# Toeplitz tiles of a causal convolution: fetched ready-made from DRAM instead of being multiplied out by GpSimd

## The chip, the cores and the metric

The kernel runs on one core of one Trainium2 chip. The metric is device time in microseconds (us) of one launch. A profile of one execution stands beside the times; all durations below come from it. Engines are called as the profile calls them: PE (TensorE, matmuls), PEld (its weight loads), DVE (VectorE), ACT (ScalarE), POOL (GpSimd), SP (SyncE, which issues most DMAs). L1809 is line 1809 of the kernel before.

## What is computed

A stack of layers on a sequence of 512 tokens and 1024 channels in fp32: a feed-forward block, a mixer of linear-recurrent heads and attention, a second feed-forward block, an "even" layer (pooling and a state-space scan), and an "odd" layer, whose mixer is cut down here to what matters:

```python
def _odd_mixer(h, w_in, conv_w, conv_b, ln_g, ln_b, w_out):
    proj = h @ w_in
    val, gt, z = proj[..., :1024], proj[..., 1024:2048], proj[..., 2048:]
    g = val * sigmoid(gt)
    c = depthwise_conv(g, conv_w, taps=31, left_pad=30) + conv_b   # per channel, causal
    c = layer_norm(c) * ln_g + ln_b
    return (silu(c) * silu(z)) @ w_out
```

The convolution has 31 taps for each of the 1024 channels. Everything has to keep fp32 accuracy, so that matrix products are done as three products of split operands (a high part `wh`, `h` and a low part `wl`), at L134, L135 and L136.

## The kernel before

The 1024 channels are 8 blocks of 128. The odd layer convolves them in two ways. Blocks 0 to 3 go tap by tap on DVE: `conv_dve` issues one instruction for tap 0 (L1786) and 30 multiply-adds (L1789, tile `cn`) for each block; these are dripped in between other work, and the layer's weight splits stand in the same in-order DVE queue (SP loads a raw tile `wr`, of which there are four buffers; L115 on ACT makes `wh` of it, L116 on DVE `wl`). Blocks 4 to 7 (`PE_BLOCKS`) go to PE as products with Toeplitz tiles: for each of the four groups of 32 channels of a block a tile `L` of 128 partitions by 36 x 32 numbers holds the taps, shifted by the phase of its partition, among zeros; 9 matmuls (L1812) run over slices of it against `G`, the flipped block. There are 16 such tiles, in four buffers (`LB` = 4), so that the four tiles of one block can be made while the block before is multiplied and no earlier than its matmuls let go of the buffers.

Before, a tile is made in two steps. During the second feed-forward block (`ffn2`), a list of side steps is taken up now and then between the matmuls; `odd_setup` is the first on it. For each of the four PE blocks it zeroes a tile on DVE (L1769), loads the taps of the block four times, shifted, by small DMAs from the ACT queue (L1772), transposes them with four PE instructions (L1776) and copies the result from PSUM (L1778) to a table `wtab`. Later, in the odd layer, POOL multiplies this table, spread over 32 columns, with a 0/1 pattern `i32` (L1809): 16 instructions of 128 x 1152 numbers, each giving one `L`. On POOL's in-order queue between them stand four additions `tot` (L1898, L1900), which sum convolved blocks for the mean of the layer norm, and small memsets of `G` (L1797).

The order in the odd layer is written out by hand (`ODD_PLAN`): `f` a block for DVE, `P6` and `P4` a projection of two PE blocks with tokens on partitions (token-major: one split weight tile serves 12 matmuls), `G` a flip, `C6`, `C7`, `C4`, `C5` the matmuls with the Toeplitz tiles, `O` the way back, `z` a gate block. After it come the mean (L1904), the layer norm (L1907, L1917) and the output projection.

The first thing in the odd layer is the norm of its input: the sums of squares (L266 on ACT, L270 on DVE) and a product with ones on PE (L284). The memory for the first four `L` comes free when the even layer's last matmuls are done.

Of the kernel before, what the change touches and what calls it, by code (L numbers as in the profile page):

```python
# [14 lines left out]
ALU = mybir.AluOpType  # L15
# [3 lines left out]
P = 128  # L19
S = 512  # L20
D = 1024
NB = D // P
# [1687 lines left out]
TAPS = 31  # L1710
# [6 lines left out]
NI = 36  # L1717
PE_BLOCKS = (4, 5, 6, 7)
# [23 lines left out]
        return R, r  # L1742


def odd_consts():
    m = (np.arange(P)[:, None] % 32 == np.arange(32)[None, :]).astype(np.float32)
    return {"k_i32": m}


def odd_setup(g, ins):  # L1750
    nc = g.nc
    g.i32 = g.c([P, 32], "i32")
    nc.scalar.dma_start(g.i32[:], ins["k_i32"])
    cw = ins["conv_w_2"].rearrange("o k c -> (o k) c")
    rows = cw.rearrange("k (b p) -> (k b) p", p=P)
    g.cw = g.c([P, TAPS, NB], "cw")
    flatw = g.cw[:].rearrange("p k b -> p (k b)")
    for i in range(2):
        t = g.b()
        nc.scalar.dma_start(t[:124, :P], rows[i * 124:(i + 1) * 124, :])  # L1760
        yield
        p = g.paux()
        nc.tensor.transpose(p[:, :124], t[:124, :P], g.ident[:124, :124])
        nc.vector.tensor_copy(flatw[:, i * 124:(i + 1) * 124], p[:, :124])
        yield
    g.wtab = {}
    for b in PE_BLOCKS:
        t = g.b()
        nc.vector.memset(t[:NI], 0.0)  # L1769
        t4 = t[:].rearrange("i (q j c) -> i q j c", q=4, j=4)  # L1770
        for j in range(4):
            nc.scalar.dma_start(t4[5 - j:36 - j, :, j, :], cw[:, b * P:(b + 1) * P].rearrange("k (q c) -> k q c", q=4))  # L1772
        yield
        p = g.paux()
        for q in range(4):
            nc.tensor.transpose(p[:, q * NI:(q + 1) * NI], t[:NI, q * P:(q + 1) * P], g.ident[:NI, :NI])  # L1776
        w = g.c([P, 4 * NI], f"wtab{b}")
        nc.vector.tensor_copy(w[:], p[:, :4 * NI])  # L1778
        g.wtab[b] = w
        yield  # L1780


def conv_dve(g, b, gp, cs):
# [19 lines left out]
def conv_pe(g, b, G):  # L1803
    nc = g.nc
    p = g.pacc()
    for q in range(4):
        L = g.X.tile([P, NI, 32], F32, tag="L", name=g.name("L"), bufs=LB)
        w = g.wtab[b][:, q * NI:(q + 1) * NI]
        nc.gpsimd.tensor_tensor(L[:], w[:, :, None].to_broadcast([P, NI, 32]), g.i32[:, None, :].to_broadcast([P, NI, 32]), ALU.mult)  # L1809
        for dc in range(9):  # L1810
            lw = L[:, (8 - dc) * 4:(8 - dc) * 4 + 4, :].rearrange("p j c -> p (j c)")
            nc.tensor.matmul(p[:, q * P:(q + 1) * P], lhsT=G[:, q, 8 - dc:8 - dc + P], rhs=lw, start=(dc == 0), stop=(dc == 8))  # L1812
    t = g.b()
    nc.scalar.activation(t[:].rearrange("p (j q c) -> p q j c", j=4, q=4), p[:].rearrange("p (q j c) -> p q j c", j=4, q=4), AF.Copy)
    return t
# [9 lines left out]
def odd(g, ins, nrm, after):  # L1825
# [51 lines left out]
    def step(op, b):  # L1877
        if op == "f":
            fm_block(b)
        elif op == "z":  # L1880
            z_block(b)
        elif op == "P":
            Zs[b // 2] = pair(b)
        elif op == "G":
            Gs[b] = conv_flip(g, b, Zs[b // 2])
        elif op == "C":
            Gs[b] = conv_pe(g, b, Gs[b])
            drip(DP)
        else:
            cs[b] = conv_out(g, b, Gs.pop(b))  # L1890
# [87 lines left out]

def all_consts():
    d = {"k_ident": np.eye(P, dtype=np.float32)}  # L1980
    for f in (mix_consts, ssm_consts, odd_consts):
        d.update(f())
    return d

# [4 lines left out]
def build(g, ins, out):  # L1989
    nc = g.nc  # L1990
    with g.region("mixc") as mixc:
        with g.region("ffn1", ring=True):
            nrm = part1(g, ins, {2: lambda: mix_loads(g, ins, mixc), 5: lambda: mix_tables(g, mixc)})
        a3 = scale_cols(g, "a3", "g_ffn2", 7)
        nrm3 = ModNorm(g, lambda: a3, modvec(g, 6))
        with g.region("mix", ring=True):
            mixer1(g, ins, nrm, modvec(g, 5), nrm3.add)
    gt3 = half_gate(g, "gt3", 8)
    with g.region("evp") as evp:
        m = Ssm(evp)  # L2000
        with g.region("ffn2", ring=True):
            def side():
                yield from odd_setup(g, ins)
                yield from ssm_prep(g, ins, m)

            nrm = EvenNorm(g)
            ffn(g, None, ins["w_gu2"], ins["w_down2"], lambda: gt3, side(), nrm.add, (0, 8, 15, 22), rate=2, side_later=PREP_LATER, nrm=nrm3)
        nrm6 = PlainNorm(g, g.cols["odd_norm_2"])
        with g.region("evm", side="left"):
            even(g, ins, nrm, m, nrm6.add)  # L2010
    with g.region("odd", side="left"):
        fin = Final(g, out)
        odd(g, ins, nrm6, fin.add)
# [18 lines left out]
```

## Time and profile before

| | |
|---|---|
| time, median of 3 runs | 1532.93 us (1531.78 to 1533.9) |
| the profiled execution's own time | 1530.95 us |
| its span, first to last instruction | 1529.2 us |
| PE busy | 1465.4 us (96%) |
| DVE busy | 1064.8 us (70%) |
| ACT busy | 637.9 us (42%) |
| POOL busy | 110.9 us (7%) |
| mean granted TensorE clock | 0.981 of full speed |

Busy time of PE is close to the span, so the time is PE's own work plus the places where PE stands still or runs at the lower clock. To read such a profile one asks first for PE's waits over the whole program, then for what the engine that PE waited for was doing, and then for the rows of the instructions that the change touches.

### The profile page before, as it was taken

What the parts mean: (1) busy time and instruction counts of PE and PEld (TensorE: products, weight loads), DVE (VectorE), ACT (ScalarE), POOL (GpSimd) and SP (SyncE); (2) the same over time, 40 slices, a digit from 0 to 9 for tenths busy, and PEclk for the clock granted to TensorE, in tenths of its full rate; (3) what the DMA queues carried; (4) which work ended last, traced back from release to release, by engine and by line L of the source; (5) the groups of instructions that cost most, each with busy time, mean ns of one, the idle gap of its engine ahead of it and who ended that gap; (6) DMA issues with size and microseconds to landing.
All of it is one profiled execution on the core that took longest, in us unless ns stands there. A gap on an engine that the chain in (4) does not pass through costs nothing.

```text
span 1529.2 us, 20513 instructions
## 1 busy us (share of the span) xinstructions
PE 1465.4 (96%) x7258; PEld 1221.0 (80%) x7258; DVE 1064.8 (70%) x2284; ACT 637.9 (42%) x1176; POOL 110.9 (7%) x118
## 2 busy tenths in 40 slices
PE   3899999999999999999999999999999998989997
PEld 3788888888987877789778888888888887869777
DVE  6885664564575687867339749946589757998975
ACT  5333223333365657845322332235434543313365
POOL 2211000000000002010000001000000002025100
PEclk7999999999999999999999999999999999999999
DMA  9498663643222213023323422332213232311121
GB/s 334 122 316 238 201 200 115 199 145 91 75 84 76 70 54 85 8 69 89 106 86 90 117 83 83 104 90 87 86 49 97 65 94 83 97 49 56 56 69 70
DMA packets 240267, 163.94 MB, mean 107 GB/s; under 512 B 18636, under 2 KB 220588, under 8 KB 240164
## 3 DMA queue, kind: packets, MB, share of 16 engines
q1 hardware_dynamic: 230260, 159.64, 34.4%
q0 software_dynamic: 1424, 1.75, 0.6%
q10 hardware_dynamic: 8480, 1.24, 0.5%
q8 instruction: 57, 0.93, 0.3%
q14 instruction: 46, 0.38, 0.1%
HBM read 159.51 MB, written 2.10 MB: 106 GB/s over the span
## 4 chain that ended last, share of the span: by engine, by line
PE 80%; DVE 12%; ACT 3%; issue 2%; DMA 2%; SPq 0%; ACTq 0%; DVEq 0%
PE pa L136 23%; PE pa L135 23%; PE pa L134 23%; DVE cn L1789 4%; DVE wl L116 1%; PE px L1076 1%; PE px L873 1%; PE px L865 1%; DVE adah L443 1%; PE pa L1812 1%; ACT wh L115 0%; DMA xt<-in_x 0%; DMA g<-in_w_gu 0%; PE px L481 0%; PE px L291 0%
## 5 line engine op out<-in xcount | busy, mean ns | idle before, releaser
L115 ACT ACTIVATE wh<-wr 128x512 fp32r<-128x512 f32 (+1 forms) x444 | 274.8, 626 | 621.4 <-PE pa L135 410.3
L116 DVE TENSOR_TENSOR wl<-wr,wh 128x512 fp32r<-128x512 f32 (+1 forms) x444 | 303.2, 688 | 242.1 <-ACT wh L115 241.1
L134 PE MATMUL pa<-h,wh 128*128 128x512 f32 (+1 forms) x1144 | 433.3, 381 | 6.1 <-ACT h L115 6.0
L136 PE MATMUL pa<-h,wl 128*128 128x512 f32 (+1 forms) x1144 | 431.1, 378 | 3.3 <-DVE wl L116 3.3
L135 PE MATMUL pa<-h,wh 128*128 128x512 f32 (+1 forms) x1144 | 431.5, 378 | 1.5 <-DVE h L116 1.5
L134 PEld LDWEIGHTS pa<-h,wh 128*128 128x128 f32 x1144 | 216.1, 189 | 45.0 <-ACT h L115 6.5
L136 PEld LDWEIGHTS pa<-h,wl 128*128 128x128 f32 x1144 | 216.4, 189 | 42.3 <-DVE wl L116 4.2
L135 PEld LDWEIGHTS pa<-h,wh 128*128 128x128 f32 x1144 | 216.9, 190 | 41.3 <-DVE h L116 3.4
L134 PE MATMUL pa<-g,wh 128*128 128x512 f32 (+1 forms) x374 | 142.3, 380 | 0.0
L135 PE MATMUL pa<-g,wh 128*128 128x512 f32 (+1 forms) x374 | 142.1, 380 | 0.0
L136 PE MATMUL pa<-g,wl 128*128 128x512 f32 (+1 forms) x374 | 141.9, 379 | 0.0
L135 PE MATMUL pa<-wl,h 128*128 128x512 f32 x256 | 102.4, 400 | 7.4 <-DVE wl L116 7.4
L1789 DVE SCALAR_TENSOR_TENSOR cn<-gp,cw,cn 128x512 f32<-128x512 f32 x120 | 105.3, 905 | 1.4
L134 PE MATMUL pa<-wh,h 128*128 128x512 f32 x256 | 103.1, 403 | 0.6 <-DVE p L1068 0.6
L136 PE MATMUL pa<-wh,h 128*128 128x512 f32 x256 | 101.6, 398 | 0.0
L136 PEld LDWEIGHTS pa<-g,wl 128*128 128x128 f32 x374 | 70.4, 188 | 12.9
L135 PEld LDWEIGHTS pa<-g,wh 128*128 128x128 f32 x374 | 70.4, 188 | 12.9
L134 PEld LDWEIGHTS pa<-g,wh 128*128 128x128 f32 x374 | 70.4, 188 | 12.6
L474 DVE SCALAR_TENSOR_TENSOR ada<-wa,cs,ada 128x1024 f32<-128x1024 f32 x49 | 62.8, 1281 | 15.0 <-DMA wa<-in_w_ada 14.6
L135 PEld LDWEIGHTS pa<-wl,h 128*128 128x128 f32 x256 | 49.2, 192 | 17.7 <-DVE wl L116 7.8
L134 PEld LDWEIGHTS pa<-wh,h 128*128 128x128 f32 x256 | 49.3, 193 | 11.1 <-DVE p L1068 1.0
L136 PEld LDWEIGHTS pa<-wh,h 128*128 128x128 f32 x256 | 49.2, 192 | 10.3
(538 smaller groups left out, 1951.0 us busy)
## 6 DMA issues: line engine op xcount, KB each, us to landing
wr<-in_w_gu SPq DMA_DIRECT2D x164, 256.0 KB
wa<-in_w_ada SPq DMA_DIRECT2D x56, 512.0 KB
wr<-in_w_down SPq DMA_DIRECT2D x64, 256.0 KB
wr<-in_w_in SPq DMA_DIRECT2D x48, 256.0 KB
g<-in_w_ada SPq DMA_DIRECT2D x32, 256.0 KB
wr<-in_even_w_in SPq DMA_DIRECT2D x32, 256.0 KB
wr<-in_odd_w_in SPq DMA_DIRECT2D x32, 256.0 KB
wr<-in_w_down SPq DMA_DIRECT2D x32, 192.0 KB
```

Source lines behind the costliest of these rows:

```text
L115: g.nc.scalar.activation(hi, src, AF.Copy)
L116: (eng or g.nc.vector).tensor_tensor(lo, src, hi.bitcast(F32), ALU.subtract)
L134: nc.tensor.matmul(out, lhsT=lh, rhs=rh, start=start, stop=False)
L135: nc.tensor.matmul(out, lhsT=lh, rhs=rl, start=False, stop=False)
L136: nc.tensor.matmul(out, lhsT=ll, rhs=rh, start=False, stop=stop)
L443: e.scalar_tensor_tensor(acc[:], t[:], s, acc[:], op0=ALU.mult, op1=ALU.add)
L474: nc.vector.scalar_tensor_tensor(acc[:], t[:], s, acc[:], op0=ALU.mult, op1=ALU.add)
L865: nc.tensor.transpose(p[:, tb * P:(tb + 1) * P], sc[tb][:, sb * P:(sb + 1) * P], g.ident[:])
L873: nc.tensor.matmul(o[:], lhsT=vv, rhs=pt[:], start=(sb == 0 and i == 0), stop=(sb == 3 and i == 1))
L1076: nc.tensor.matmul(o[:, d, :], lhsT=ex[d][j][:, ts], rhs=v1[j][:, hd, :], start=(j == js[0]), stop=(j == js[-1]))
L1789: nc.vector.scalar_tensor_tensor(c[:], gp[:, k:k + S], g.cw[:, k, b:b + 1], c[:], op0=ALU.mult, op1=ALU.add)
L1812: nc.tensor.matmul(p[:, q * P:(q + 1) * P], lhsT=G[:, q, 8 - dc:8 - dc + P], rhs=lw, start=(dc == 0), stop=(dc == 8))
```

## The change

The host lays out all 16 Toeplitz tiles, zeros included, in a new DRAM input `k_convw` of 2048 rows by 1152 numbers (9.4 MB). The pattern `i32`, the tables `wtab` and the steps that made them go; the list of side steps gets eight empty steps in their place, so that the steps behind them come at the same places of `ffn2`. Each POOL multiplication L1809 becomes a DMA of 128 x 1152 numbers (576 KB) from POOL's queue into the same tile.

```diff
+def conv_layout(w):
+    w = w.reshape(TAPS, NB, 4, 32)[:, list(PE_BLOCKS)]
+    out = np.zeros((len(PE_BLOCKS), 4, 4, 32, NI, 32), np.float32)
+    for j in range(4):
+        for c in range(32):
+            out[:, :, j, c, 5 - j:36 - j, c] = w[:, :, :, c].transpose(1, 2, 0)
+    return {"k_convw": out.reshape(len(PE_BLOCKS) * 4 * P, NI * 32)}
 def odd_setup(g, ins):
-    g.i32 = g.c([P, 32], "i32")
-    nc.scalar.dma_start(g.i32[:], ins["k_i32"])
...
-    g.wtab = {}
-    for b in PE_BLOCKS:
-        t = g.b()
-        nc.vector.memset(t[:NI], 0.0)
-        t4 = t[:].rearrange("i (q j c) -> i q j c", q=4, j=4)
-        for j in range(4):
-            nc.scalar.dma_start(t4[5 - j:36 - j, :, j, :], cw[:, b * P:(b + 1) * P].rearrange("k (q c) -> k q c", q=4))
-        yield
-        p = g.paux()
-        for q in range(4):
-            nc.tensor.transpose(p[:, q * NI:(q + 1) * NI], t[:NI, q * P:(q + 1) * P], g.ident[:NI, :NI])
-        w = g.c([P, 4 * NI], f"wtab{b}")
-        nc.vector.tensor_copy(w[:], p[:, :4 * NI])
-        g.wtab[b] = w
-        yield
+    g.convw = ins["k_convw"]
+    yield from [None] * (2 * len(PE_BLOCKS))
 def conv_pe(g, b, G):
-        w = g.wtab[b][:, q * NI:(q + 1) * NI]
-        nc.gpsimd.tensor_tensor(L[:], w[:, :, None].to_broadcast([P, NI, 32]), g.i32[:, None, :].to_broadcast([P, NI, 32]), ALU.mult)
+        r = (PE_BLOCKS.index(b) * 4 + q) * P
+        nc.gpsimd.dma_start(L[:].rearrange("p i c -> p (i c)"), g.convw[r:r + P, :])
```

On PE, in `ffn2`, the first of four places with transposes stands like this before (`px` and `t` are the transposes' target and source, `pa` a sum of the feed-forward block, `h` its input, `wh` and `wl` split weights):

```order
3419 L136 MATMUL pa_7199<-h_6552,wl_7195 128x512
3420 L1776 MATMUL px_7086<-ident,t_7080 128x36
3421 L134 MATMUL pa_7236<-h_6538,wh_7225 128x512
3422 L1776 MATMUL px_7086<-ident,t_7080 128x36
3423 L135 MATMUL pa_7236<-h_6539,wh_7225 128x512
3424 L1776 MATMUL px_7086<-ident,t_7080 128x36
3425 L136 MATMUL pa_7236<-h_6538,wl_7226 128x512
3426 L1776 MATMUL px_7086<-ident,t_7080 128x36
3427 L134 MATMUL pa_7236<-h_6540,wh_7225 128x512
3428 L135 MATMUL pa_7236<-h_6541,wh_7225 128x512
```

The change takes these 16 instructions out of PE's row, four at each of four places, one between each two matmuls, and moves no other of PE's instructions; the matmuls around them then follow one another without a break. On DVE the four memsets and four copies go, and the two copies of L1764 come a little later among the splits; on ACT the 16 small DMA issues and that of `i32` go, and the small DMAs of the next side steps come some splits earlier. In the odd layer DVE's, ACT's and PE's rows are the same as before.

On POOL, from the second block's tiles (C7) to the third's (C4), this stands before (`c` are convolved blocks):

```order
98 L1809 TENSOR_TENSOR L_12997<-wtab_7373,i_6942 128x1152
99 L1809 TENSOR_TENSOR L_13008<-wtab_7373,i_6942 128x1152
100 L1809 TENSOR_TENSOR L_13019<-wtab_7373,i_6942 128x1152
101 L1809 TENSOR_TENSOR L_13030<-wtab_7373,i_6942 128x1152
102 L1797 MEMSET G_13051 128x4x8
103 L1898 TENSOR_TENSOR tot_13468<-c_12994,c_12889 128x512
104 L1809 TENSOR_TENSOR L_13109<-wtab_7091,i_6942 128x1152
```

and this after, at the same place of POOL's row:

```order
98 L1798 DMA L_12943<-in_k_convw 128x1152
99 L1798 DMA L_12954<-in_k_convw 128x1152
100 L1798 DMA L_12965<-in_k_convw 128x1152
101 L1798 DMA L_12976<-in_k_convw 128x1152
102 L1786 MEMSET G_12997 128x4x8
103 L1887 TENSOR_TENSOR tot_13414<-c_12940,c_12835 128x512
104 L1798 DMA L_13055<-in_k_convw 128x1152
```

The DMAs take the places of the multiplications one for one; the additions and memsets between them stay where they were.

## Rows read from the trace of the kernel before

**Rows 1.** What PE waited for, whole program: engine, line, releaser, us, times, longest.

```profile
PE pa L135 <- DVE wl L116: 7.4, 1, 7.4
...
PE px L284 <- DVE t L270: 4.9, 1, 4.9
...
PE px L1904 <- ACT c L1791: 1.1, 1, 1.1
```

**Rows 2.** POOL in order of time, odd layer: start us, us, instruction, [idle before].

```profile
1272.81 9.73 POOL L1809 TENSOR_TENSOR L<-wtab,i 128x1152 f32<-128x1152 f32 x4
...
1350.61 10.24 POOL L1809 TENSOR_TENSOR L<-wtab,i 128x1152 f32<-128x1152 f32 x4 [68.01 <-PE pa L1812]
...
1391.98 9.75 POOL L1809 TENSOR_TENSOR L<-wtab,i 128x1152 f32<-128x1152 f32 x4
```

**Rows 3.** DVE in order of time beside the first four builds.

```profile
1273.26 2.23 DVE L116 TENSOR_TENSOR wl<-wr,wh 128x512 fp32r<-128x512 f32 x1
...
1275.53 2.49 DVE L1584 SCALAR_TENSOR_TENSOR h<-x,cols,h 128x512 fp32r<-128x512 f32 x1
1277.94 2.61 DVE L270 TENSOR_TENSOR t<-t,t 128x512 f32<-128x512 f32 x1
```

**Rows 4.** PE after its first wait; last row the same product later, without a wait.

```profile
1280.70 1.84 PE L284 MATMUL px<-ones,t 128*128 128x1 f32 x8 [4.89 <-DVE t L270]
...
1286.19 0.40 PE L136 MATMUL pa<-h,wl 128*128 128x512 f32 x1
...
1458.66 0.95 PE L284 MATMUL px<-ones,t 128*128 128x1 f32 x8
```

**Rows 5.** DVE and PE in order of time around the second wait.

```profile
1353.71 7.69 DVE L1789 SCALAR_TENSOR_TENSOR cn<-gp,cw,cn 128x512 f32<-128x512 f32 x3
...
1364.63 4.71 DVE L1789 SCALAR_TENSOR_TENSOR cn<-gp,cw,cn 128x512 f32<-128x512 f32 x7
...
1370.00 0.79 PE L135 MATMUL pa<-wl,h 128*128 128x512 f32 x1 [7.37 <-DVE wl L116]
...
1374.79 0.40 PE L134 MATMUL pa<-wh,h 128*128 128x512 f32 x1
```

**Rows 6.** Ten us of all engines: busy (and count), PEclk, DMA share, GB/s.

```profile
1360.00:1370.00 10.00, 2.63 (x12) 1.86 (x10) 10.00 (x15) 0.98 (x2) 0.91 (x2) 0.89 0.00 0
```

**Rows 7.** DVE during P4, after the second wait: weight splits.

```profile
1378.50 0.69 DVE L116 TENSOR_TENSOR wl<-wr,wh 128x512 fp32r<-128x512 f32 x1
...
1381.34 0.68 DVE L116 TENSOR_TENSOR wl<-wr,wh 128x512 fp32r<-128x512 f32 x1
```

**Rows 8.** The transposes in `ffn2`: their summary, and PE around the first four.

```profile
L1776 PE MATMUL px<-ident,t x16: 248/248/250, 751.7 to 790.8; 36*128 36x36 f32 x16
...
750.43 0.39 PE L135 MATMUL pa<-h,wh 128*128 128x512 f32 x1
...
751.34 0.39 PE L136 MATMUL pa<-h,wl 128*128 128x512 f32 x1
...
753.99 0.39 PE L135 MATMUL pa<-h,wh 128*128 128x512 f32 x1
```

**Rows 9.** The Toeplitz matmuls of C7 and of C4 on PE.

```profile
1388.88 8.20 PE L1812 MATMUL pa<-L,G 128*128 128x128 f32 x72
...
1403.27 8.20 PE L1812 MATMUL pa<-L,G 128*128 128x128 f32 x72
```

**Rows 10.** DMAs from POOL's queue: us to landing; DVE beside them; the stretch, columns as rows 6.

```profile
amask<-in_k_amask POOLq DMA_DIRECT2D x1, 448.0 KB, 6.1
...
g<-g POOLq DMA_DIRECT2D x8, 128.0 KB, 3.0
...
109.93 1.28 DVE L474 SCALAR_TENSOR_TENSOR ada<-wa,cs,ada 128x1024 f32<-128x1024 f32 x1
...
125.34 1.29 DVE L474 SCALAR_TENSOR_TENSOR ada<-wa,cs,ada 128x1024 f32<-128x1024 f32 x1 [1.66 <-DMA wa<-in_w_ada]
...
108.00:112.00 4.00, 4.00 (x20) 3.27 (x19) 3.97 (x18) 1.24 (x2) 3.10 (x6) 1.00 0.97 309
```

More of the change, by code (lines that the diff above doesn't have):

```diff
@@ L1742, in finish @@
         return R, r
-def odd_consts():
-    m = (np.arange(P)[:, None] % 32 == np.arange(32)[None, :]).astype(np.float32)
-    return {"k_i32": m}
+def conv_layout(w):
[5 more added lines that the diff above has]
+    return {"k_convw": out.reshape(len(PE_BLOCKS) * 4 * P, NI * 32)}
 def odd_setup(g, ins):
     nc = g.nc
-    g.i32 = g.c([P, 32], "i32")
-    nc.scalar.dma_start(g.i32[:], ins["k_i32"])
     cw = ins["conv_w_2"].rearrange("o k c -> (o k) c")
@@ L1980, in all_consts @@
     d = {"k_ident": np.eye(P, dtype=np.float32)}
-    for f in (mix_consts, ssm_consts, odd_consts):
+    for f in (mix_consts, ssm_consts):
         d.update(f())
@@ L2021 @@
     data.update(all_consts())
+    data.update(conv_layout(data["conv_w_2"]))
     nc = bacc.Bacc("TRN2", target_bir_lowering=False, num_devices=1)
```

## The prediction

> **What bounds the kernel now.** PE is busy for 96% of the span, so I read first what PE waited for over the whole program, and picked the waits in the stretch that the change touches [rows 1]: three, of 7.4, 4.9 and 1.1 us. In `ffn2`, where the side steps run, the same view has no wait of PE at all; there an instruction that leaves PE's queue is worth what it takes there. Next I read POOL in order of time, because the two long waits name DVE, and DVE's own work in these places has not grown. POOL builds four tiles in one go from 1272.81, four more from 1350.61 and eight from 1391.98 on, of which the first four have a row [rows 2], about 2.5 us each. Beside the first four, DVE's instructions of 128 x 512 take 2.23, 2.49 and 2.61 us [rows 3]; without them a split, the same kind of instruction, takes 0.68 or 0.69 us [rows 7], and a multiply-add 4.71 / 7 = 0.67 us [rows 5]. Beside the second four, a multiply-add takes 7.69 / 3 = 2.56 us [rows 5], as long as one tile on POOL. So while POOL multiplies, DVE gets through about one instruction per tile: the two take turns. DVE is then full (10.00 of 10 us) while PE does 2.63 us of work [rows 6]. The builds cost nothing on POOL itself; they cost time through DVE.
>
> **The change part by part.**
>
> *Transposes in `ffn2`.* Sixteen go [rows 8]. PE's matmuls there follow each other every 0.2275 us (four steps from 750.43 to 751.34). From 751.34 to 753.99, with four transposes in between, five steps took 2.65 us in place of 1.14: 1.51 us for a place, 6.0 us for four. The transposes' own 16 x 0.248 = 4.0 us is the lower bound; the rest is the break they make in the pipeline of matmuls. Nothing late stands behind PE in that stretch, so it all goes: **-6.0**. The eight small DVE instructions and the 17 DMA issues on ACT stood beside a full PE and are worth nothing to the end.
>
> *First wait, even to odd.* PE waits 4.89 us for the last addition L270 of the sum of squares [rows 4]. DVE's three instructions ahead, one after the other, are longer by (2.23 + 2.49 + 2.61) - 3 x 0.7 = 5.2 us [rows 3]. At their free length the sum is ready when PE gets there, so the wait goes. After it PE runs at the lower of its two clock levels: from 1280.70 to 1286.19 it does L284 and nine steps of matmuls in 5.49 us; L284 takes 0.95 us at full clock (last row of rows 4) and nine steps 2.05, so 2.49 us were the clock's. Without the wait there is no reason for the drop: **-7.4**.
>
> *Second wait, in P4.* L135 waits 7.37 us for a weight split that stands on DVE behind 17 multiply-adds [rows 5]. Four of these fell beside the builds and lost 4 x (2.56 - 0.67) = 7.5 us. The split is then done just when PE needs it, with nothing to spare. PE's slow matmuls after the wait, 11 steps in 4.79 us (1370.00 to 1374.79), cost 4.79 - 11 x 0.2275 = 2.29 us more, so 9.66 in all. I give part of it back: in P4 a split and three multiply-adds take DVE 2.84 us [rows 7], while PE uses up one split weight tile in 12 x 0.2275 = 2.73. Before, the long wait had given DVE a lead; without it PE waits about 0.1 us for most of the eight tiles. I take 0.6 and bound it at 1.5: **-9.0**.
>
> *Third wait.* The mean waits 1.1 us for the last block of DVE's convolution [rows 1], which runs beside the last eight builds and would be several us earlier without them: **-1.1**. The chain of the layer norm behind it starts at PE's mean as before.
>
> *The DMAs.* Sixteen of 576 KB go out from POOL at the places of the builds. The trace has no such DMA. The nearest from this queue are one of 448 KB, landing after 6.1 us in a stretch where the DMA engines are full (0.97), and eight of 128 KB at 3.0 us [rows 10]; the odd layer's share goes down to 0.00 [rows 6]. I take 5 us, bounds 3.0 and 6.1 x 576 / 448 = 7.8. The shortest time to hide it is from C7 to C4: a buffer comes free during C7 and is needed at the same point of C4, 1403.27 - 1388.88 = 14.4 us later, [rows 9]. POOL's first addition `tot` stands ahead of them and is done by 1391.98, 3.1 us after C7 began [rows 2], which leaves 11 us for the first tile. The four overlap, so all land in time: 0. A wait of POOL's queue for a buffer delays only its own additions `tot`, which the mean needs much later. Issuing is cheap for DVE as well: six issues took POOL 3.10 us (last stretch of [rows 10]), and the multiply-add L474 between them took 1.28 us, as the one after them 1.29. The weight loads from SP share the DMA engines; they have four buffers ahead, some 11 us at one tile per 2.73. I take 0, with 3 us as the worse end.
>
> A page states the price directly. The Trainium skill, "DMA: Bandwidth & Descriptors", section "Anatomy of one DMA — SWDGE (gpsimd) path", gives about 2.0 us and the bytes at 436 GB/s; that would be an estimated 3.4 us for a tile, and the sum would stay. No run here shows that rate: the last row of rows 10 moves 309 GB/s.
>
> Sum: 6.0 + 7.4 + 9.0 + 1.1 = 23.5 us. The profiled execution took 1530.95, so 1507.4 would be its like; the median of the runs is 1532.93, 1.98 above it. I forecast 1509.
>
> **Rivals.**
>
> *The tiles land late (slower).* If the four DMAs of a block ran one behind the other at d us each, those for C4, which start once C7 lets go and the first `tot` is done (1392, rows 2), would end at 1392 + 4d; the last is needed three quarters into C4, at 1403.27 + 6.15 = 1409.4 [rows 9]. PE would stop for 4d - 17.4 us, and 2.3 more at the low clock as in rows 5. At d = 7.8 that is 16.1, leaving about 1525; it decides against the change from 4d - 17.4 + 2.3 = 23.5, d = 9.7. C5's tiles would add a stop of their own, which I don't price. At d = 11 the time is about 1509 + 28.9 = 1538. For it: DVE is full in this stretch, POOL has never moved tiles of this size here, and the 6.1 us. Against it: the DMA engines are almost idle here, six issues went out back to back beside a DVE busy for 3.97 of 4 us [rows 10], and they overlapped in flight. Chance 0.06, and 0.04 for the smaller loss that ends within 0.2% of before.
>
> The Trainium skill has a rule for this, in "SBUF — State Buffer", section "SBUF: two separate sides": a DVE instruction in a two-port mode keeps GpSimd from writing the descriptors of its DMAs, and a DMA of 620 ns alone took 3100 beside such instructions. Five times the 3.0 us of rows 10 would be an estimated 15 us for a tile and a time well above 1560. The trace disagrees as far as it goes (last row of rows 10), and the multiply-adds have two inputs, where the page speaks of copies and the like; I leave this in the 0.06.
>
> *DVE takes over as the bound (a smaller gain).* Once PE no longer stands still at 1362, DVE has to serve P4 with no lead, full as it is [rows 6]. If the split came later than I think, by one or two multiply-adds and their tiles, PE would stop several times for 1 to 2 us and drop its clock once: 5 to 8 us less gain, 1514 to 1517. For it: 2.84 against 2.73. Against it: the 7.5 us that DVE gains are those which the split was late by. Chance 0.15.
>
> *The transposes were not worth it, or the edges keep their waits.* If only the 4.0 us of rows 8 comes back and the first wait shrinks by half, the gain is 23.5 - 2.0 - 3.7, and the time 1515. Chance 0.10.
>
> **How the numbers follow.** The forecast, 1505 to 1513, has 0.65; DVE as the bound 0.15; smaller terms 0.10; a late tile that eats the gain 0.04; slower 0.06. The range 1504 to 1520 leaves out the last two, and some room for what I have not seen. This kernel's measurement tells about 0.2%, 3 us, from no change. Faster by more than that 0.90, within it 0.04, slower 0.06.
>
> **What would show it.** Right: in `ffn2` PE's matmuls run through at 0.2275 us where the transposes were; no instruction of DVE of 2.5 us beside the POOL DMAs; L284 of the odd norm without a wait; L135 in P4 with waits under 1 us; the granted clock at full from 1260 to 1450; each tile's landing well under 12 us. Wrong: L1812's first matmul in C7, C4 or C5 waiting for a DMA; L1789 still above 1 us beside an issue; a new wait of PE in P4 for L116, of several us, with DVE full. I would be wrong most simply if the DMAs for C4 took over 9 us each.

## The result, and the profile after

| | before | after |
|---|---|---|
| time, median | 1533.16 us (1531.78 to 1533.9, 4 runs) | 1509.4 us (1506.55 to 1512.18, 4 runs) |
| ratio, 95% interval | 1 | 0.9846 (0.9825 to 0.9866) |
| profiled execution, span | 1529.2 us | 1508.4 us |
| PE busy | 1465.4 us | 1456.5 us |
| DVE busy | 1064.8 us | 1038.5 us |
| POOL busy | 110.9 us | 85.6 us |
| mean granted TensorE clock | 0.981 | 0.985 |

The change gains 23.8 us. From L1768 on, lines now carry numbers that are 11 lower: the multiply-add is L1778 (before L1789), the Toeplitz matmul L1801 (L1812), the DMA that took the build's place L1798 (L1809). What PE waits for, whole program (engine, line, releaser: us, times, longest):

```profile
PE px L452 <- DVE adah L443: 13.4, 1, 13.4
PE pa L134 <- ACT h L115: 6.0, 2, 3.0
...
PE pa L135 <- DVE h L116: 1.8, 4, 0.9
...
PE px L173 <- ACT t L1541: 1.4, 1, 1.4
```

The three waits of [rows 1] are gone; between 1265 and 1445 us the view lists no wait of PE at all. What remains is mostly the start of the program and the norms. The last line is new: the kernel before has no wait at L173. It ends at 1158.57 us, in the even layer, which the change does not touch, and is followed up below. POOL in order of time, odd layer (start, us, instruction, [idle before]):

```profile
1271.14 2.18 POOL L1798 DMA_DIRECT2D L<-in_k_convw  x4 [0.38 <-issue]
...
1341.11 0.53 POOL L1798 DMA_DIRECT2D L<-in_k_convw  x1 [67.65 <-PE pa L1801]
...
1371.22 2.12 POOL L1887 TENSOR_TENSOR tot<-c,c 128x512 f32<-128x512 f32 x1 [23.42 <-ACT c L1810]
1373.28 0.57 POOL L1798 DMA_DIRECT2D L<-in_k_convw  x1
```

Where [rows 2] has four builds in 9.73 us, four issues take 2.18. They stand at the same places and wait for the same buffers. DVE beside the first four, against [rows 3]:

```profile
1271.16 0.69 DVE L116 TENSOR_TENSOR wl<-wr,wh 128x512 fp32r<-128x512 f32 x1
...
1272.04 0.75 DVE L1584 SCALAR_TENSOR_TENSOR h<-x,cols,h 128x512 fp32r<-128x512 f32 x1
1272.71 0.69 DVE L270 TENSOR_TENSOR t<-t,t 128x512 f32<-128x512 f32 x1
```

and PE, against [rows 4]:

```profile
1273.57 1.00 PE L284 MATMUL px<-ones,t 128*128 128x1 f32 x8
```

2.23, 2.49 and 2.61 us have become 0.69, 0.75 and 0.69; L284 comes without a wait and at full clock. DVE ahead of P4's first split and PE there, against [rows 5]:

```profile
1340.89 11.35 DVE L1778 SCALAR_TENSOR_TENSOR cn<-gp,cw,cn 128x512 f32<-128x512 f32 x17
1352.14 0.70 DVE L116 TENSOR_TENSOR wl<-wr,wh 128x512 fp32r<-128x512 f32 x1
```

```profile
1352.57 0.39 PE L134 MATMUL pa<-wh,h 128*128 128x512 f32 x1
1352.89 0.50 PE L135 MATMUL pa<-wl,h 128*128 128x512 f32 x1
```

All 17 multiply-adds now take 11.35 / 17 = 0.67 us, the last ones and the first alike, although POOL issues four DMAs beside them. The split ends at 1352.84 and L135 starts at 1352.89, a tenth of a us later than it would without any wait. All engines in the same stretch and in the first one with DMAs (busy, PEclk, DMA share, GB/s, columns as in [rows 6]):

```profile
1270.00:1280.00 10.00, 10.00 (x53) 8.37 (x52) 5.70 (x17) 5.80 (x9) 2.44 (x6) 1.00 0.87 307
1340.00:1350.00 10.00, 10.00 (x79) 9.52 (x78) 10.00 (x16) 1.09 (x2) 2.24 (x5) 1.00 0.74 225
1350.00:1360.00 10.00, 10.00 (x45) 8.01 (x44) 9.89 (x16) 2.54 (x4) 0.00 (x0) 1.00 0.34 112
```

PE is busy for 10.00 of 10 us with the clock at 1.00 in each; before, [rows 6] had 2.63 and a clock of 0.89. The last view is the summary of the tile `L`:

```profile
L1798 POOL DMA_DIRECT2D L<-in_k_convw x16: 527/528/602, 1271.1 to 1392.7; - x16
...
DMA to landing us min/median/max: 4.0/4.9/7.8
```

In `ffn2`, PE's matmuls run through where the transposes stood (in [rows 8], five steps of matmuls took 2.65 us there; here one takes 0.22 or 0.23):

```profile
754.07 0.39 PE L134 MATMUL pa<-h,wh 128*128 128x512 f32 x1
754.29 0.39 PE L135 MATMUL pa<-h,wh 128*128 128x512 f32 x1
754.52 0.39 PE L136 MATMUL pa<-h,wl 128*128 128x512 f32 x1
```

**Where the time went, stage by stage.** PE's instructions are the same in all kernels here but for the transposes, so each can be looked up in two traces and its starts subtracted. The table gives, for each kernel's profiled execution, how much of the difference to the kernel before arises in each stage (us, median over the instructions at the stage's two ends; minus is a gain); "L173" is the stretch from 1145 to 1200 us, and the last column is what is left of the difference between the spans, in stretches that the change does not touch. The names of the other kernels are explained with their experiments.

| kernel | start, to 200 | transposes | L173 | first wait | second wait | third wait | elsewhere |
|---|---|---|---|---|---|---|---|
| after | +2.5 | -6.2 | +1.6 | -7.5 | -9.5 | -1.5 | 0.0 |
| after, second execution | -0.3 | -6.2 | +1.8 | -7.6 | -9.5 | -1.5 | -0.5 |
| preparation put back | +0.1 | 0.0 | 0.0 | -7.6 | -9.5 | -1.5 | -1.5 |
| first block by DMA | +4.5 | 0.0 | 0.0 | -7.6 | +0.4 | +0.1 | 0.0 |
| other blocks by DMA | +0.1 | 0.0 | 0.0 | 0.0 | -9.5 | -1.6 | -0.5 |
| memset ahead of each DMA | +1.9 | -6.3 | +1.1 | -7.6 | -9.5 | -1.5 | +0.7 |
| build ahead of each DMA | -0.6 | -6.2 | +1.4 | +3.9 | +1.2 | +0.3 | +0.1 |

Where an edit takes a wait or the transposes away, the gain repeats to 0.1 us, whichever kernel it comes from.

The column L173 is a loss that comes with the transposes' gain: it is there in every kernel of the table without the preparation, and in none with it. On ACT, the first split behind a pause of the weight loads stands like this before

```profile
1152.32 0.64 ACT L115 ACTIVATE wh<-wr 128x512 fp32r<-128x512 f32 x1 [2.84 <-DMA wr<-in_even_w_in]
```

and like this after:

```profile
1150.55 0.63 ACT L115 ACTIVATE wh<-wr 128x512 fp32r<-128x512 f32 x1 [4.80 <-DMA wr<-in_even_w_in]
```

SP issued that load at 1149.34 before and at 1145.63 after, 3.7 us earlier like PE's instructions there; but from its issue to the split it took 4.9 us instead of 3.0. Behind it DVE stands idle for 1.61 us, as it does not before, and ACT's L1541, for which PE waits, comes late with the rest. Why the load takes longer is not shown.

The first column does not repeat: it is between -0.6 and +4.5, and +2.5 and -0.3 in two executions of the same kernel. There PE waits some 3 us at 46 to 49 us, and the clock after it differs. Six us behind that wait, columns as above, of before:

```profile
50.00:56.00 6.00, 6.00 (x36) 5.18 (x34) 4.21 (x8) 0.00 (x0) 0.00 (x0) 1.00 0.00 0
```

of after:

```profile
50.00:56.00 6.00, 6.00 (x25) 4.96 (x24) 3.77 (x8) 0.00 (x0) 0.00 (x0) 0.72 0.00 0
```

and of the kernel with only the first block by DMA:

```profile
50.00:56.00 6.00, 6.00 (x20) 5.06 (x19) 2.79 (x7) 0.00 (x0) 0.00 (x0) 0.50 0.00 0
```

36, 25 and 20 instructions in the same 6 us at clocks of 1.00, 0.72 and 0.50. So the pair of profiled executions shows 20.8 us and the medians 23.8: the 2.5 at the start are one execution's luck and no cost of the change, as the second execution's -0.3 shows.

### The profile page after: what moved, and what is told of

Read it like the earlier page. It is cut to its first block, busy times and chain, and to the rows that moved or that the text cites. A ratio compares the mean times of both kernels' runs of the same rounds, so it can differ in the third digit from the quotient of the medians.

```text
span 1508.4 us, 20447 instructions
## 1 busy us (share of the span) xinstructions
PE 1456.5 (97%) x7242; PEld 1217.5 (81%) x7242; DVE 1038.5 (69%) x2276; ACT 639.6 (42%) x1176; POOL 85.6 (6%) x118
## 4 chain that ended last, share of the span: by engine, by line
PE 87%; DVE 7%; DMA 2%; ACT 2%; issue 1%; SPq 1%; ACTq 0%; DVEq 0%
PE pa L135 25%; PE pa L136 25%; PE pa L134 25%; PE pa L1801 2%; DMA g<-in_w_ada 1%; PE px L1076 1%; PE px L873 1%; DVE cn L1778 1%; DVE wl L116 1%; PE px L865 1%; PE px L173 0%; PE px L136 0%; PE px L134 0%; PE px L135 0%; PE px L481 0%
## 5 line engine op out<-in xcount | busy, mean ns | idle before, releaser
L116 DVE TENSOR_TENSOR wl<-wr,wh 128x512 fp32r<-128x512 f32 (+1 forms) x444 | 299.1, 679 | 238.4 <-ACT wh L115 237.5
L135 PE MATMUL pa<-h,wh 128*128 128x512 f32 (+1 forms) x1144 | 430.7, 377 | 1.9 <-DVE h L116 1.8
L135 PEld LDWEIGHTS pa<-h,wh 128*128 128x128 f32 x1144 | 216.5, 189 | 41.6 <-DVE h L116 3.9
L135 PE MATMUL pa<-g,wh 128*128 128x512 f32 (+1 forms) x374 | 142.1, 380 | 0.0
L135 PE MATMUL pa<-wl,h 128*128 128x512 f32 x256 | 101.6, 397 | 0.0
L1778 DVE SCALAR_TENSOR_TENSOR cn<-gp,cw,cn 128x512 f32<-128x512 f32 x120 | 89.0, 770 | 1.5
L135 PEld LDWEIGHTS pa<-g,wh 128*128 128x128 f32 x374 | 70.4, 188 | 12.8
L544 DVE TENSOR_TENSOR s<-s,pa 128x512 f32<-128x512 f32 x43 | 29.5, 687 | 42.3 <-PE pa L136 41.0
L134 PEld LDWEIGHTS pa<-wh,h 128*128 128x128 f32 x256 | 48.7, 190 | 10.9 <-DVE p L1068 1.0
L135 PEld LDWEIGHTS pa<-wl,h 128*128 128x128 f32 x256 | 48.7, 190 | 10.5 <-DVE wl L116 0.8
```

The costliest lines, as they stand in the source:

```text
L116: (eng or g.nc.vector).tensor_tensor(lo, src, hi.bitcast(F32), ALU.subtract)
L134: nc.tensor.matmul(out, lhsT=lh, rhs=rh, start=start, stop=False)
L135: nc.tensor.matmul(out, lhsT=lh, rhs=rl, start=False, stop=False)
L544: nc.vector.tensor_tensor(s[:], s[:], pu[:], ALU.mult)
L1778: nc.vector.scalar_tensor_tensor(c[:], gp[:, k:k + S], g.cw[:, k, b:b + 1], c[:], op0=ALU.mult, op1=ALU.add)
```

## The experiments

**The preparation put back.** The changed kernel, with the removed steps of `odd_setup` instead of the eight empty ones.

```diff
-    yield from [None] * (2 * len(PE_BLOCKS))
+    g.wtab = {}
+    for b in PE_BLOCKS:
+        t = g.b()
+        nc.vector.memset(t[:NI], 0.0)
...
+        g.wtab[b] = w
+        yield
```

> The changed kernel, with the preparation in ffn2 put back: memsets, small DMAs, 16 transposes and copies, whose tables nobody reads; the 16 tiles still come by DMA. My theory: the transposes cost 6.0 us (1.5 at each of four places), so 1515.4. If only their own 4.0 us counted, 1513.4. If they were hidden, 1509.4, and the gain came from the odd layer alone.

Measured: 1515.29 us (1510.99 to 1517.67), ratio to before 0.9887 (0.9872 to 0.9901). By the medians the preparation costs 5.9 us. In the table the stage of its transposes goes from -6.2 to 0.0, so they were not hidden, and they cost more than their own 4.0 us. But the loss at L173 goes too, from +1.6 to 0.0 (the load takes 2.9 us here), so that the preparation is worth only 4.6 us net in the traces; the four times, 1510.99 to 1517.67, can't tell that from 5.9.

**Only the first block, and only the others.** The kernel before, with both ways of making a tile.

```diff
-        w = g.wtab[b][:, q * NI:(q + 1) * NI]
-        nc.gpsimd.tensor_tensor(L[:], ...)
+        if b == 6:      # the other kernel: b != 6
+            r = (PE_BLOCKS.index(b) * 4 + q) * P
+            nc.gpsimd.dma_start(L[:].rearrange("p i c -> p (i c)"), g.convw[r:r + P, :])
+        else:
+            w = g.wtab[b][:, q * NI:(q + 1) * NI]
+            nc.gpsimd.tensor_tensor(L[:], ...)
```

> The kernel before, with the first block's four tiles (C6) by DMA; the other twelve are still multiplied out by POOL, and the preparation stays. My theory: the wait of L284 and its slow clock go, 7.4 us: 1525.5; DVE's 2.5 us instructions beside the first four builds are gone, those in P4 are still there. Rival, the wait only moves to P4 because DVE is the bound there: about 1531.

> The reverse: the first four tiles are multiplied out by POOL, the other twelve come by DMA, and the preparation stays. My theory: the second and third wait go, 9.0 + 1.1 us: 1522.8, and the wait of L284 stays at about 4.9 us. Rival, DVE late in P4 whatever POOL does: the second wait stays in part, 1527 or more. If the parts add, the gains of this run, of the one with the first block alone and of the transposes (6.0) come to the whole 23.5.

Measured: 1526.52 us (1523.7 to 1528.49), ratio 0.9962 (0.995 to 0.9974), and 1518.52 us (1517.2 to 1523.09), ratio 0.9916 (0.9902 to 0.9929). PE's waits in the odd layer that belong here, of the first kernel (L1918 is the mean, L1904 before):

```profile
PE pa L135 <- DVE wl L116: 7.4, 1, 7.4
PE px L1918 <- ACT c L1801: 1.3, 1, 1.3
```

and of the second:

```profile
PE px L284 <- DVE t L270: 4.9, 1, 4.9
```

Each wait follows its own block's builds: the first goes with the first four, the second and third with the others, and the ones that are left keep their length to 0.2 us. The rival that the first wait only moves on to P4 falls. The medians miss the expected times by +1.0 and -4.3 us; the table says where that is. In the first kernel the start was 4.5 us late in the profiled execution. In the second the second wait was worth 9.5 and not 9.0, the third 1.6 and not 1.1, and the kernel before, run beside it, had a median of 1531.79, 1.1 us under the one that I had reckoned from. The rest of the 4.3 us, about 2.2, lies in no stage that the change touches. One source of such scatter stands in the traces: for six us behind PE's wait of 3.0 us in the last norm, the granted clock was 0.72 in the execution of before and 1.00 in this one, and PE gains 1.6 us there. The two gains and that of the transposes, by medians 5.3 + 13.3 + 5.9 = 24.5, come to the whole 23.8 within the scatter.

**POOL's multiplication with nobody waiting for it.** The changed kernel, and behind each DMA a multiplication into a tile `U` that nobody reads.

```diff
+        U = g.X.tile([P, NI, 32], F32, tag="U", name=g.name("U"), bufs=1)
+        w = g.cw[:].rearrange("p k b -> p (k b)")[:, q * NI:(q + 1) * NI]
+        nc.gpsimd.tensor_tensor(U[:], w[:, :, None].to_broadcast([P, NI, 32]), g.ident[:, None, :32].to_broadcast([P, NI, 32]), ALU.mult)
```

> The changed kernel, with a POOL multiplication of the same size (128 x 1152, two inputs spread from SBUF) behind each of the 16 DMAs; its result goes to a tile that nobody reads. My theory: the builds cost time through DVE, not through their result, so nearly all of the odd layer's 17.5 us comes back: 1524 to 1527, with DVE instructions of 2.5 us beside them. Rival, PE or DVE waited for what the builds wrote: 1509 to 1510.

Measured: 1532.2 us (1527.43 to 1535.15), ratio 1.0001 (0.9991 to 1.0011). The gain is gone to the last us, but not at the old places. Nothing held the later twelve multiplications back, so they ran in one go:

```profile
1280.60 29.53 POOL L1801 TENSOR_TENSOR U<-cw,ident 128x1152 f32<-128x1152 f32 x12
```

and the three longest waits of PE in the odd layer are

```profile
PE pa L134 <- ACT wh L115: 13.0, 1, 13.0
PE px L284 <- DVE t L270: 3.6, 1, 3.6
PE pa L135 <- DVE wl L116: 1.1, 1, 1.1
```

DVE in the same stretch, in order of time:

```profile
1303.00 7.67 DVE L1778 SCALAR_TENSOR_TENSOR cn<-gp,cw,cn 128x512 f32<-128x512 f32 x3
```

That is 2.56 us each, as in [rows 5]. So nobody has to need POOL's result for the loss; it falls on whatever PE next wants from DVE (here, through DVE's splits and ACT, 13 us at 1299 to 1312). As a test of the old places it was badly laid, which the next two mend.

**Writing without reading, and the old build again.** The changed kernel, with POOL writing each tile before its DMA overwrites it: once by two memsets, once by one multiplication. The tile ties them to the old places.

```diff
+        nc.gpsimd.memset(L[:], 0.0)
+        nc.gpsimd.memset(L[:], 1.0)
```

```diff
+        w = g.cw[:].rearrange("p k b -> p (k b)")[:, q * NI:(q + 1) * NI]
+        nc.gpsimd.tensor_tensor(L[:], w[:, :, None].to_broadcast([P, NI, 32]), g.ident[:, None, :32].to_broadcast([P, NI, 32]), ALU.mult)
```

> The changed kernel, with two POOL memsets of each tile L (128 x 1152) ahead of its DMA, which then overwrites it: POOL works at the places of the old builds, but only writes SBUF. My theory: DVE loses time beside a POOL instruction that reads SBUF, not beside one that only writes it; 1509 to 1511, and multiply-adds of 0.7 to 0.8 us beside the memsets. The Trainium skill has this rule in SBUF — State Buffer, section Who interferes with whom. Rival, any POOL work in SBUF holds DVE up: up to the 18.5 us of the traces' three waits (7.3 + 9.6 + 1.6) come back, so 1520 to 1528.

> The same with one POOL multiplication of the old builds' size in place of the two memsets: it reads two spread inputs, writes the tile, and the DMA overwrites it. Theory: all three waits come back, 1509.4 + 18.5 = 1528, and DVE's instructions beside it take 2.5 us. Rival, the waits came from who needs the result: 1509 to 1512, as the DMA still brings the tile within its 11 us.

Measured: 1510.11 us (1509.55 to 1510.77), ratio 0.9853 (0.9839 to 0.9868), with memsets; 1532.26 us (1528.53 to 1534.21), ratio 0.9992 (0.9981 to 1.0003), with multiplications. POOL in order of time in the first kernel, at C7's tiles:

```profile
1339.66 1.06 POOL L1797 MEMSET L<- 128x1152 f32 x1 [59.80 <-PE pa L1803]
1340.77 1.06 POOL L1798 MEMSET L<- 128x1152 f32 x1
```

and DVE there:

```profile
1339.69 11.35 DVE L1778 SCALAR_TENSOR_TENSOR cn<-gp,cw,cn 128x512 f32<-128x512 f32 x17
```

POOL in the second kernel, at the same tiles:

```profile
1349.02 2.70 POOL L1798 TENSOR_TENSOR L<-cw,ident 128x1152 f32<-128x1152 f32 x1 [70.47 <-PE pa L1803]
```

and DVE:

```profile
1348.99 16.13 DVE L1778 SCALAR_TENSOR_TENSOR cn<-gp,cw,cn 128x512 f32<-128x512 f32 x11
```

Beside eight memsets of 1 us DVE's 17 multiply-adds take 11.35 us, to the digit what they take beside nothing but DMA issues. Beside four multiplications eleven take 16.13, 1.47 each on average (the last builds end at 1359.9, so not all eleven stand beside one), and all 17 take 20.10 us, against 18.84 before. PE's two waits are back (7.7 and 8.7 us, before 4.9 and 7.4). The kernel with memsets has one short wait of its own, 1.2 us for the last tile of C4, whose DMA POOL issues only at 1385.14 (1378.30 in the changed kernel). Reading is what matters: the multiplication and the memset write the same tile, and only the first reads SBUF. That is the rule of the Trainium skill, "SBUF — State Buffer", section "SBUF: two separate sides": a DVE instruction with two SBUF inputs and a GpSimd instruction that reads SBUF exclude each other for the whole of an instruction. The traces agree, with 0.67 us against 2.5. The second kernel is 4 us slower than I expected: one L270 took 5.41 us, twice the 2.61 of [rows 3], and the 17 multiply-adds 1.26 us more than before; so the first wait grew by 2.8 us and the second by 1.3 over before. That the DMA issues between the multiplications stretch them so is likely, but not shown.

**How late may a tile be?** Once each tile is fetched twice, the second time behind the first's landing; once there are three buffers instead of four.

```diff
         nc.gpsimd.dma_start(L[:].rearrange("p i c -> p (i c)"), g.convw[r:r + P, :])
+        nc.gpsimd.dma_start(L[:].rearrange("p i c -> p (i c)"), g.convw[r:r + P, :])
```

```diff
-LB = 4
+LB = 3
```

> The changed kernel, with each tile fetched twice, the second DMA behind the first's landing: traffic and time to readiness doubled. By POOL's order of DMAs and a landing of 5 us, the last tile of C4 would be there about 1394, 3.5 us after it is needed: 1513 to 1516, with a wait of PE for a DMA in C4. Rival, the slack is larger than the 11 us I worked out: 1509 to 1511. Rival, the queue is much slower with twice the descriptors: over 1525.

> The changed kernel, with three buffers for L instead of four; PE's, DVE's and ACT's orders stay. A block's last tile then has to wait for the buffer of its first: it is free 2.05 us after the block begins and needed at 6.15, so 4.1 us are there for an issue of 0.5 and a landing of 4 to 5. Theory: PE waits about 1.3 us in each of the four blocks, and may lose its clock: 1514 to 1520. Rival, landing on an idle queue is under 4 us: 1509 to 1511.

Measured: 1512.4 us (1507.49 to 1515.81), ratio 0.9876 (0.9854 to 0.9897), and 1512.54 us (1511.27 to 1515.26), ratio 0.9872 (0.9857 to 0.9886). PE's waits for tiles, in the first, where the matmul is L1802:

```profile
PE pa L1802 <- DMA L<-in_k_convw: 2.1, 2, 1.7
```

and in the second:

```profile
PE pa L1801 <- DMA L<-in_k_convw: 4.1, 4, 2.2
```

Both medians lie 3 us above the changed kernel's 1509.4, below the ranges that I expected (from 1513 and from 1514), and the first kernel's times scatter from 1507.49 to 1515.81. The traces have the losses at the places expected: with tiles fetched twice PE is 2.6 us late in C4; with three buffers it waits for the last tile of each of the four blocks, 0.4 to 2.2 us, and is 5.2 us late in all (this execution, 1515.26, was the slowest of its four). The slack of the four buffers is real but not large: a landing twice as long begins to show. The clock was 1.00 in the 10 us around the longest stop of 2.2 us, so the part "and may lose its clock" did not come.

**More of the same in `ffn2`.** The changed kernel, with the taps (L1765) and four inputs of the state-space scan laid out by the host; on top of it, the first additions of the program on DVE instead of POOL; and the changed kernel itself again.

```diff
+    nc.scalar.dma_start(g.cw[:].rearrange("p k b -> p (k b)"), ins["k_cw"])
...
+    nc.scalar.dma_start(c[:], ins["k_ssm"])
...
+    nc.scalar.dma_start(ct.rearrange("p r q h -> p (r q h)"), ins["k_ct"])
```

```diff
-    ada_half(g, sh, 0, 0, [nc.gpsimd, nc.vector])
+    ada_half(g, sh, 0, 0, [nc.vector])
```

> The changed kernel, with the other weights that only needed another layout in ffn2 (the taps, and four inputs of the state-space scan) laid out by the host too: 12 more fp32 transposes leave PE's queue there. Theory: each costs what those of the change did, 6.0 / 16 = 0.38 us, so 4.5 us: 1505. Rival, only their own busy time, about 0.25 us each: 1506.4. Rival, ffn2 is no longer full of PE work: 1509.

> That kernel, and in the first microseconds POOL's three additions L446 of the first half of the modulation, which stand beside DVE's L443, done by DVE. PE waits 13.4 us for that sum. There, ten L443 and the merge of the two sums took DVE 10.86 + 0.69 us; fourteen at 0.74 are 10.4. Theory (POOL reading SBUF blocks DVE here too, and DVE sets the end): 1 to 2 us less than the one with more layouts, 1503.5. Rival, the loads of the weights set the end of the sum: no difference.

> The changed kernel itself, beside the two with further steps on the same chip: 1509.4 as in its first runs, within 2 us.

Measured: 1512.14 us (1510.91 to 1513.51), ratio 0.9862 (0.9844 to 0.988); 1511.03 us (1508.43 to 1512.92), ratio 0.9856 (0.9838 to 0.9875); and the changed kernel 1508.26 us (1504.53 to 1510.72), ratio 0.9837 (0.9816 to 0.9859). Taking twelve more transposes out made the kernel no faster, rather some us slower. The trace of the kernel with twelve gone has a new wait of PE, the only long one in `ffn2`:

```profile
PE pa L134 <- ACT g L115: 3.9, 1, 3.9
```

and the ten us in which it begins, columns as above, look like this:

```profile
790.00:800.00 10.00, 7.19 (x32) 5.63 (x30) 9.71 (x52) 0.84 (x2) 0.00 (x0) 1.00 0.26 80
```

In the changed kernel DVE is busy for 5.24 of these 10 us and PE for 10.00. Without transposes to wait for, the scan's small DVE instructions moved up by some 78 us (the first of one group from 854.3 to 776.8) into the last gate blocks, where PE needs `s` and `g` from DVE and ACT at once. By the starts of PE's instructions the stop and the slow clock behind it cost 5.0 us. The theory was wrong in its price too, as the next run shows. The additions on DVE shortened PE's first wait from 13.6 to 12.4 us, as expected, but another of 2.9 us, for a split on POOL, came up behind it; a difference of 1.1 us between the two medians is within their scatter.

The last kernel takes ten out: the edits on `cw` and `ct` above stand, the one on `ssmc` is undone (shown against the kernel with twelve gone), so that the scan's two transposes of 16 and 48 partitions stay.

```diff
-    nc.scalar.dma_start(c[:], ins["k_ssm"])
+    p = g.paux()
+    nc.tensor.transpose(p[:, :16], t[:16, :P], g.ident[:16, :16])
...
+    nc.tensor.transpose(p[:, :48], rows[:48, :P], g.ident[:48, :48])
```

> The changed kernel with ten of the twelve transposes gone (the two of the taps and the eight of the scan's output weights), but the small columns of the scan prepared as before, two transposes included. In the kernel with twelve gone, the scan's small DVE instructions had moved up into the last gate blocks of ffn2, where PE then waited 3.9 us for a split of g and lost its clock for another 1.4. Theory: with the scan's first two transposes in place its steps keep their place, that wait is gone, and ten transposes are worth 3.8 us: 1505. Rival, the scan's later steps pile up on DVE somewhere else in ffn2: no gain, 1509 to 1512.

Measured: 1507.53 us (1506.94 to 1510.42), ratio 0.9846 (0.9826 to 0.9866). The wait is gone, as expected, but the gain of 3.8 us did not come: this kernel can't be told from the changed one. From the first of the ten to the last, its PE gains 1.25 us on the changed kernel's. (It gains 1.6 more where the changed kernel waits at L173: here the load takes 3.1 us again, and the wait is gone. The medians don't resolve either.) The reason stands in the trace of after, where four of these transposes are still there:

```profile
906.95 0.39 PE L136 MATMUL pa<-h,wl 128*128 128x512 f32 x1
907.18 0.27 PE L1398 MATMUL px<-ident,t 128*64 128x128 f32 x1
907.21 0.47 PE L134 MATMUL pa<-h,wh 128*128 128x512 f32 x1
907.52 0.27 PE L1398 MATMUL px<-ident,t 128*64 128x128 f32 x1
...
908.55 0.39 PE L135 MATMUL pa<-h,wh 128*128 128x512 f32 x1
```

Five steps of matmuls from 906.95 to 908.55 take 1.60 us instead of 1.14, so a transpose of 128 partitions costs 0.12 us, and ten 1.2; that of 36 partitions cost 0.38 [rows 8]. I had carried a price over from one shape to another.

## Why the prediction was right

It gave 1509.0 and the median was 1509.4. The mechanism was right, and each of the four gains holds by itself, a little larger than forecast. That the total is so near is in part luck: a loss that the prediction did not have, the wait at L173, takes back what the gains were too small by.

*Transposes:* -6.0, and 6.2 to 6.3 in the traces. The choice of 1.51 us for a place, from the steps of the matmuls around it, over the transposes' own 4.0 us was right. Wrong was "Nothing late stands behind PE in that stretch, so it all goes": some 400 us further on a load comes late, and 1.6 us of the gain is lost there.

*First wait:* -7.4, and 7.5. Both parts came: the wait of 4.9 and the slow clock behind it.

*Second wait:* -9.0, and 9.5. Of the 0.6 that I gave back because DVE would serve P4 with no lead, about 0.2 came: at first a round of DVE takes 2.59 us there (1352.14 to 1354.73, next split), less than PE's 2.73, and of the later rounds of 2.85 PE feels a tenth or less. The rival in which DVE takes over as the bound had the same step and falls with it.

*Third wait:* -1.1, and 1.5. The layer norm's chain moved with the mean; what the 0.4 beyond the wait itself are is not shown.

*DMAs:* 0, and no wait of PE for a tile. The landing taken as 5 us has a median of 4.9; the bound of 7.8 was just the longest. The estimate of 3.4 us from the Trainium skill, "DMA: Bandwidth & Descriptors", section "Anatomy of one DMA — SWDGE (gpsimd) path", is short of all 16 (the shortest is 4.0). Five times as long, by the rule on starved descriptors of the Trainium skill, "SBUF — State Buffer", section "SBUF: two separate sides", was not seen: an issue took POOL 0.53 us, and the four tiles at 1341 to 1348, where DVE is full, landed after 4.3 to 5.0. The page states that rule for a DVE instruction in a two-port mode, so two-input multiply-adds do not test it. (By the prediction's own 4d - 17.4 + 2.3, its 15 us a tile would have made 1554, not well above 1560.) The rival of late tiles, one behind the other, did not come: the first four, issued within 2.18 us, landed 4.2 to 7.8 us after their issue. That late tiles cost PE time is right, only far off: twice the fetching lost 2.6 us in C4.

The four gains of the table make 24.7 us instead of 23.5, and 23.1 with the loss at L173. The profiled pair shows only 20.8, because of the start of that execution, and the second execution of after shows 23.7 by the end of the program. The mechanism, that POOL's reading of SBUF takes DVE's turns, was argued from the trace before; the memsets and multiplications ahead of the DMAs have shown it.

## What to carry to other kernels

An engine that is 7% busy can still set the time, if its instructions take turns with those of a full one: look at what the durations of the full engine's instructions do beside it. Price work that you take out of a queue by the gap it leaves between its neighbours, for just that shape, and not by its own duration or that of a relative. And ask where the steps go that were waiting for it: removing twelve cheap transposes let small instructions move up to a place where DVE had no time for them. Then follow the gain to the end of the program: of the 6.2 us in `ffn2`, 1.6 were lost again at a weight load far behind it.

## What was not expected

- A transpose of few partitions between full matmuls is dearer than a full one: 0.38 us at 36 partitions (four places), 0.36 and 0.39 at 16 and 48 (one each), 0.12 at 128. They also have fewer columns (36 x 36 against 128 x 128), so which of the two it is stays open. The Trainium skill, "TensorEngine Tiling (Array Packing)", section "Key Properties", says that changing the tiling mode drains TensorE; that would fit, but no run shows that the small ones use another mode.
- A stop of PE of about 3 us was followed by the lower clock in some executions of the same kernel and not in others (0.72 and 1.00 in two executions of after), worth 2.8 us at the start between these two and up to 5.1 between the traces of the table; a stop of 2.2 us in the run with three buffers left the clock at 1.00.
- DVE's two-input instructions took the same 0.67 us beside POOL's memsets as beside its DMA issues, so an engine that only fills tiles costs DVE nothing here.
- One weight load of the even layer took 4.1 to 5.1 us from its issue to its split in all seven traces of kernels that lack the 16 transposes and keep the twelve others, and 2.8 to 3.1 in the other seven. No run here says why.
